# Sampled attention beside a main stream: when keys are turned, when values are gathered, and how the value products stand on TensorE

## The chip, the cores and the metric

The kernel runs on one core of a Trainium2 chip. The metric is device time in microseconds (us) of one execution; below, "before" and "after" are the kernel without and with the change. Engine names in the profile: PE is TensorE (PEld its weight loads), DVE is VectorE, ACT is ScalarE, POOL is GpSimd, SP is SyncE, which here issues most DMAs.

## What is computed

One inference step of a one-layer decoder. A prompt of 2048 new tokens and eight sampled sequences with eight new tokens each go through one input projection, two mixers (FoX attention with forget gates, and an mLSTM with matrix memory), an output projection with layer norm and an MLP with a squared ReLU and a second norm. All data are float32. The part that the change touches is the FoX attention of the sampled tokens over 8192 past tokens per sequence, which lie in pages of 128 tokens, found through a page table:

```python
def _fox_sample(q, k_new, v_new, logf_new, k_past, v_past, logf_past):
    ...
    s_past = jnp.einsum('bqhd,bkhd->bhqk', q, k_past).astype(jnp.float32) * scale
    s_past = s_past + Ln[..., :, None] + R[:, :, None, :]
    s_new = jnp.einsum('bqhd,bkhd->bhqk', q, k_new).astype(jnp.float32) * scale
    ...
    p = jax.nn.softmax(jnp.concatenate([s_past, s_new], axis=-1), axis=-1).astype(v_new.dtype)
    o = jnp.einsum('bhqk,bkhd->bqhd', p[..., :P], v_past) + jnp.einsum('bhqk,bkhd->bqhd', p[..., P:], v_new)
```

Here b is one of 8 sequences, q one of 8 tokens, h one of 8 heads and d one of 64 channels; R is the forget sum from a past token to the end of the past.

## The kernel before, in words

**The main stream.** Four phases follow each other: A (input projection, with the mLSTM beside it), B (prompt attention, `phase_b`), O (output projection, `phase_o`) and C (MLP, `phase_c`). Their large products run in three terms of split numbers through `mm3` (L137 to L140): a high and a low part of each operand, as 128x512 or 128x256 matmuls on the whole 128x128 array.

**The side stream.** The sampled attention is a generator, `sample_attention`, that runs beside phases A, O and C. The main stream calls `tick(us)` after its products with the microseconds that they are thought to take; whenever enough have come together (7.5 us in phase A, 5 us in O and C, never in B), `beside` makes one step of the generator, and the step's instructions on PE, ACT and DVE are put behind the main stream's latest instruction on that engine. A scheduler that works out the order of every engine at build time may still move a step's instructions among the main stream's. On the chip each engine then keeps that order and waits at each instruction for what it needs. POOL and SP are not tied to the main stream: they run ahead until a buffer is not free.

**A step before.** For sequence b, 16 key tiles of 512 tokens are worked through in pairs, each pair in four steps. A step calls `k_step(b, kt, m)` for the current sequence and `pv_step(b - 1, kt + m // 2, m % 2)` for the one before it.

- `k_step` (L1304): a gather from POOL (L1314, an indirect DMA of 512 KB into `kraw`, two buffers), and at once, in the same step, two 128x512 transposes on DVE (L1316) from `kraw` into `kT` (one buffer). The first of four steps also loads the forget sums `Rb` from SP (L1311).
- `qk_step` (L1318), after each fourth step: 16 matmuls of 128x32 weights against 256 columns (L1327); the query tokens of four heads lie in four column quarters of the array, so four matmuls in a row go to four quarters. DVE adds the forget sums and takes the maximum (L1334).
- `softmax` (L1338), after a sequence's last tile: 16 small matmuls (L1345), the maximum, exponentials on ACT, the row sums.
- `weights` (L1381), for each fourth of the tiles: transposes of the weights (L1388) and copies to `PTs` (L1390).
- `pv_step` (L1393): a gather of 512 KB of values into `vt` (L1401, two buffers) and in the same step the four matmuls that use it (L1406), again in four column quarters, all into one accumulator `sO` that is kept for the whole sequence. The last one of a sequence also adds the new tokens' values (L1411) and puts the result out (L1414 to L1423).

So each step has two gathers, and a gather of values may start as soon as PE has used the last value but one. The attention of the last sequence needs one more round of steps without keys.

## Time and profile before

| what | before |
|---|---|
| time, median of 3 runs (lowest to highest) | 3501.9 us (3501.55 to 3503.35) |
| profiled execution: span from first to last instruction | 3492.4 us |
| median of the runs less that span | 9.5 us |
| phase A, from the start | about 1000 us |
| phase B | about 443 us |
| phase O | about 217 us |
| phase C to the end of the sampled attention | about 1300 us |
| the rest of phase C | about 532 us |
| mean granted clock of TensorE | 0.985 |

The profile gives the span of one profiled execution; its time outside the span is not recorded by itself, and the 9.5 us to the median of the runs stand for it. A group row reads: line, engine, operation, out<-in, shape (128*32 means 128 rows and 32 columns of the array), count, busy time and mean ns. A timeline row reads: start and duration in us, engine, line, operation, names, shape, count of equal instructions in a row, and in brackets the engine's idle time before it with what ended it. A float32 matmul of the sampled attention leaves two records, one of the main stream leaves one. A wait row reads: who waited, on which line, for whom, then us in total, number of times and the longest.

### The profile page before, as it was taken

How to read it: one execution, taken by the hardware profiler on the slowest of the kernel's cores; microseconds unless marked ns; L12 is line 12 of the kernel's file. 1: busy time of each engine (PE TensorE's matmuls, PEld its weight loads, DVE VectorE, ACT ScalarE, POOL GpSimd, SP SyncE). 2: the span in 40 equal slices, each digit the busy share in tenths (PEclk: the TensorE clock that was granted, in tenths of full speed). 3: DMA queues.
4: the chain of work that ended last, by engine and by line, in shares of the span. 5: the costliest groups of instructions: out<-in, count | busy, mean ns of one | idle time of the engine just before them, and what ended most of it. 6: DMA issues, size and time to landing. Idle time of an engine off the chain costs nothing.

```text
span 3492.4 us, 59522 instructions
## 1 busy us (share of the span) xinstructions
PE 3354.9 (96%) x22428; PEld 2670.1 (76%) x22428; DVE 2178.9 (62%) x5302; ACT 1366.6 (39%) x2818; POOL 897.4 (26%) x942
## 2 busy tenths in 40 slices
PE   8899899999989999999899999999999999999998
PEld 8898778888866666667567677677677777898887
DVE  6747747657558787655556567666666544654555
ACT  3333323334358888512324243332233333443332
POOL 1013213231322222265332324223324111100000
PEclk9999999999999999999899999999999999999999
DMA  6557777775853232586776767768768555442221
GB/s 198 167 167 223 223 220 237 245 246 174 275 163 86 75 81 57 172 275 215 273 250 197 266 214 262 258 200 271 253 218 296 192 164 176 148 154 73 85 85 64
DMA packets 446040, 663.15 MB, mean 190 GB/s; under 512 B 84604, under 2 KB 333760, under 8 KB 444856
## 3 DMA queue, kind: packets, MB, share of 16 engines
q1 hardware_dynamic: 369064, 380.13, 36.1%
q0 software_dynamic: 74304, 270.57, 22.5%
q10 hardware_dynamic: 2384, 8.65, 0.7%
q8 instruction: 176, 2.88, 0.3%
q14 instruction: 112, 0.92, 0.1%
HBM read 598.01 MB, written 61.22 MB: 189 GB/s over the span
## 4 chain that ended last, share of the span: by engine, by line
PE 69%; DMA 15%; DVE 6%; issue 5%; POOL 3%; ACT 1%; SPq 0%; POOLq 0%; DVEq 0%; ACTq 0%
PE py L138 7%; PE py L140 6%; PE py L139 6%; PE ph L138 6%; PE ph L139 6%; PE ph L140 6%; DMA kraw<-cache_k,idxK 4%; PE po L919 4%; DMA vt<-cache_v,idxV 4%; PE pt L910 4%; PE pm L138 4%; PE pm L139 3%; PE pm L140 3%; PE sO L1406 3%; PE pS L871 2%
## 5 line engine op out<-in xcount | busy, mean ns | idle before, releaser
L1150 DVE TENSOR_TENSOR y<-y,py 128x512 f32<-128x512 f32 (+1 forms) x476 | 319.3, 680 | 251.1 <-PE py L140 246.9
L138 PE MATMUL ph<-x1h,wh 128*128 128x512 f32 (+1 forms) x1280 | 455.5, 356 | 2.4 <-ACT wh L130 2.4
L130 ACT ACTIVATE wh<-wr 128x1024 fp32r<-128x1024 f32 x264 | 273.4, 1057 | 466.0 <-PE py L140 264.0
L139 PE MATMUL ph<-x1l,wh 128*128 128x512 f32 (+1 forms) x1280 | 454.7, 355 | 0.0
L140 PE MATMUL ph<-x1h,wl 128*128 128x512 f32 (+1 forms) x1280 | 453.7, 355 | 0.2 <-DVE wl L133 0.2
L1401 POOL DMA_INDIRECT vt<-cache_v,idxV x256 | 257.9, 1007 | 736.1 <-PE sO L1406 701.2
L1316 DVE STREAM_TRANSPOSE kT<-kraw 128x512 f32<-128x512 f32 x512 | 328.3, 684 | 179.8 <-DMA kraw<-cache_k,idxK 178.4
L138 PE MATMUL py<-wh,hh 128*128 128x512 f32 (+1 forms) x1088 | 431.6, 399 | 1.5 <-DVE y L1148 0.8
L139 PE MATMUL py<-wl,hh 128*128 128x512 f32 (+1 forms) x1088 | 429.6, 395 | 0.7 <-DVE wl L133 0.7
L140 PE MATMUL py<-wh,hl 128*128 128x512 f32 (+1 forms) x1088 | 429.1, 395 | 0.0
L1314 POOL DMA_INDIRECT kraw<-cache_k,idxK x256 | 280.9, 1097 | 571.3 <-DVE kT L1316 439.0
L133 DVE TENSOR_TENSOR wl<-wr,wh 128x1024 fp32r<-128x1024 f32 x264 | 333.2, 1269 | 91.4 <-PE ph L140 25.7
L138 PE MATMUL pm<-whi,xh 128*128 128x256 f32 (+2 forms) x1088 | 320.3, 294 | 7.5 <-DVE st L489 4.8
L139 PE MATMUL pm<-wlo,xh 128*128 128x256 f32 (+2 forms) x1088 | 315.7, 290 | 0.0
L140 PE MATMUL pm<-whi,xl 128*128 128x256 f32 (+2 forms) x1088 | 315.4, 290 | 0.0
L138 PEld LDWEIGHTS ph<-x1h,wh 128*128 128x128 f32 x1280 | 240.9, 188 | 46.5 <-issue 11.1
L140 PEld LDWEIGHTS ph<-x1h,wl 128*128 128x128 f32 x1280 | 240.7, 188 | 42.8 <-issue 11.1
L139 PEld LDWEIGHTS ph<-x1l,wh 128*128 128x128 f32 x1280 | 240.6, 188 | 40.4 <-issue 8.6
L138 PEld LDWEIGHTS py<-wh,hh 128*128 128x128 f32 (+1 forms) x1088 | 201.3, 185 | 62.7 <-issue 18.1
L140 PEld LDWEIGHTS py<-wh,hl 128*128 128x128 f32 (+1 forms) x1088 | 201.3, 185 | 55.5 <-issue 9.9
L139 PEld LDWEIGHTS py<-wl,hh 128*128 128x128 f32 (+1 forms) x1088 | 201.5, 185 | 48.5 <-issue 8.6
L138 PE MATMUL pm<-xh,whi 128*128 128x256 f32 (+1 forms) x768 | 224.7, 293 | 0.8 <-ACT qi L447 0.8
(359 smaller groups left out, 6875.1 us busy)
## 6 DMA issues: line engine op xcount, KB each, us to landing
wr<-w SPq DMA_DIRECT2D x256, 512.0 KB
wra<-w_in SPq DMA_DIRECT2D x112, 512.0 KB
xn<-x_prompt SPq DMA_DIRECT2D x32, 512.0 KB
Rb<-dR SPq DMA_DIRECT2D x128, 128.0 KB
dqk<-th SPq DMA_DIRECT2D x32, 256.0 KB
qk<-dqk SPq DMA_DIRECT2D x16, 512.0 KB
qn<-dq SPq DMA_DIRECT2D x128, 64.0 KB
wr<-w_o SPq DMA_DIRECT2D x16, 512.0 KB
```

Of the source, the lines that this page charges most:

```text
L130: last["ACT"] = A.activation(dst, src, AF.Copy, scale=scale)
L133: r = (eng or V).tensor_tensor(dst, src, hi.bitcast(F32), op=OP.subtract)
L138: T.matmul(ps, wh, xh, start=first, stop=False)
L139: T.matmul(ps, wh, xl, start=False, stop=False)
L140: last["PE"] = T.matmul(ps, wl, xh, start=False, stop=stop)
L910: T.transpose(pt[:, k], sc[i][0][k0 // 4][:, k * 128:(k + 1) * 128], ident)
L919: last["PE"] = T.matmul(po[c:c + 64, q0:], z["vn"][:, k], PT[:, k - k0, q0:], start=(k < 2), stop=(k >= nk - 2), skip_group_check=True)
L1150: V.tensor_tensor(y, y, ps, op=OP.add)
L1314: G.indirect_dma_start(out=kraw, out_offset=None, in_=ck, in_offset=IO(ap=idxK[:, b, kt + k, f:f + 1], axis=0))
L1316: V.transpose(z["kT"][:, k, 2 * f + i].rearrange("p b c -> p (b c)"), kraw[:, i * 512:(i + 1) * 512])
L1401: G.indirect_dma_start(out=vt.rearrange("p f c -> p (f c)"), out_offset=None, in_=cv, in_offset=IO(ap=idxV[:, b, pg * 4 + u, f:f + 1], axi ...
L1406: T.matmul(po[r:r + 32], z["PT"][:, hg, 2 * f + g, pg].rearrange("p h q -> p (h q)"), vt[:, g, hg * 256:(hg + 1) * 256], start=(kt == 0 an ...
```

## The change

The generator's nested loops become a chain of 291 numbered steps, `step(n)`, one for each call by the main stream. In step n:

- the keys that step n - 1 gathered are turned (`k_turn`); every fourth step the score products follow (`qk_step`), and after a sequence's last tile the softmax;
- then the next 512 KB of keys are gathered (`k_gather`, with the load of `Rb` in each fourth step). `kraw` still has two buffers and `kT` one;
- in every second step, the value products of 512 tokens are made (`pv_step`): eight matmuls in place of twice four. The second gathered half comes first (f = 1, then f = 0). `tc.issue_after` puts the first four behind the last score product of the same step, if there is one, and the other four behind the first four;
- right behind them both halves of the next 512 values are gathered (`v_gather`), which the products two steps later use. `vt` still has two buffers. The new tokens' values (`v_new`) are loaded with a sequence's first gather of values instead of in `qk_begin`, and the transposed weights of a fourth of the tiles (`weights`) follow the gather of its first values.

The number of gathers, transposes, matmuls, copies and buffers is the same. `pv_end` is the old end of `pv_step` as a function. Comments and docstrings are gone elsewhere, which moves line numbers and nothing else. The core of the diff:

```diff
-        vn = ps_.tile([8, 512], F32, name="vns", bufs=1)
-        SY.dma_start(vn, O["v_sample"][0, b].rearrange("t h d -> t (h d)"))
...
-    def k_step(b, kt, m):
+    def k_gather(b, j):
         z = state[b]
-        if m == 0:
-            z["kT"] = ps_.tile([128, 2, 4, 16, 32], F32, name="kT", tag="kT", bufs=1)
+        kt, f = j // 2, j % 2
+        z["kraw"] = ps_.tile([128, 1024], F32, name="kraw", tag="kraw", bufs=2)
+        G.indirect_dma_start(out=z["kraw"], out_offset=None, in_=ck, in_offset=IO(ap=idxK[:, b, kt, f:f + 1], axis=0))
+        if j % 4 == 0:
             z["rb"] = ps_.tile([128, 2, 256], F32, name="Rb", bufs=1)
             for hg in range(2):
                 SY.dma_start(z["rb"][:, hg], dap(dR, (b * FH + hg * 4) * PAST + kt * 128, [[2048, 16], [0, 8], [1, 256]]))
-        k, f = divmod(m, 2)
-        kraw = ps_.tile([128, 1024], F32, name="kraw", tag="kraw", bufs=2)
-        G.indirect_dma_start(out=kraw, out_offset=None, in_=ck, in_offset=IO(ap=idxK[:, b, kt + k, f:f + 1], axis=0))
+
+    def k_turn(b, j):
+        z = state[b]
+        if j % 4 == 0:
+            z["kT"] = ps_.tile([128, 2, 4, 16, 32], F32, name="kT", tag="kT", bufs=1)
+        k, f = divmod(j % 4, 2)
         for i in range(2):
-            V.transpose(z["kT"][:, k, 2 * f + i].rearrange("p b c -> p (b c)"), kraw[:, i * 512:(i + 1) * 512])
+            V.transpose(z["kT"][:, k, 2 * f + i].rearrange("p b c -> p (b c)"), z["kraw"][:, i * 512:(i + 1) * 512])
...
-    def pv_step(b, kt, f):
+    def v_gather(b, kt):
         z = state[b]
-        if kt == 0 and f == 0:
+        z["vt"] = []
+        for f in range(2):
+            vt = ps_.tile([128, 2, 512], F32, name="vt", bufs=2)
+            G.indirect_dma_start(out=vt.rearrange("p f c -> p (f c)"), out_offset=None, in_=cv,
+                                 in_offset=IO(ap=idxV[:, b, (kt % 4) * 4 + kt // 4, f:f + 1], axis=0))
+            z["vt"].append(vt)
+
+    def pv_step(b, kt, after):
+        z = state[b]
+        if kt == 0:
             z["po"] = pps.tile([128, 256], F32, name="sO", bufs=1)
         po = z["po"]
-        u, pg = divmod(kt, 4)
-        vt = ps_.tile([128, 2, 512], F32, name="vt", bufs=2)
-        G.indirect_dma_start(out=vt.rearrange("p f c -> p (f c)"), out_offset=None, in_=cv,
-                             in_offset=IO(ap=idxV[:, b, pg * 4 + u, f:f + 1], axis=0))
-        for g in range(2):
-            for hg in range(2):
-                r = (g * 2 + hg) * 32
-                T.matmul(po[r:r + 32], z["PT"][:, hg, 2 * f + g, pg].rearrange("p h q -> p (h q)"),
-                         vt[:, g, hg * 256:(hg + 1) * 256], start=(kt == 0 and f == 0),
-                         stop=(g == 1 and kt == 15 and f == 1), skip_group_check=True)
+        pg = kt % 4
+        for n, f in enumerate((1, 0)):
+            with ExitStack() as es:
+                if after is not None:
+                    es.enter_context(tc.issue_after(after.ins))
+                for g in range(2):
+                    for hg in range(2):
+                        r = (g * 2 + hg) * 32
+                        after_ = T.matmul(po[r:r + 32], z["PT"][:, hg, 2 * f + g, pg].rearrange("p h q -> p (h q)"),
+                                          z["vt"][f][:, g, hg * 256:(hg + 1) * 256], start=(kt == 0 and n == 0),
+                                          stop=(g == 1 and kt == 15 and n == 1), skip_group_check=True)
+            after = after_
+        if kt == 15:
+            pv_end(b, po)
...
-    yield 1
-    for b in range(9):
-        if b < 8:
-            qk_begin(b)
-        for kt in range(0, 16, 2):
-            if b > 0 and kt % 4 == 0:
-                weights(b - 1, kt // 4)
-            for m in range(4):
-                yield 1
-                if b < 8:
-                    k_step(b, kt, m)
-                if b > 0:
-                    pv_step(b - 1, kt + m // 2, m % 2)
-            if b < 8:
-                qk_step(b, kt)
+    def step(n):
+        after = None
+        b, j = divmod(n, 32)
+        kb, kj = divmod(n - 1, 32)
+        vb, vj = divmod(n - 36, 32)
+        if 0 <= kb < 8:
+            k_turn(kb, kj)
+            if j % 4 == 0:
+                after = qk_step(kb, kj // 4 * 2)
+                if j == 0:
+                    softmax(kb)
         if b < 8:
-            softmax(b)
+            if j == 0:
+                qk_begin(b)
+            k_gather(b, j)
+        if n % 2 == 0:
+            if 0 <= vb < 8:
+                pv_step(vb, vj // 2, after)
+            wb, wj = divmod(n - 34, 32)
+            if 0 <= wb < 8:
+                v_gather(wb, wj // 2)
+                if wj == 0:
+                    v_new(wb)
+                if wj % 8 == 0:
+                    weights(wb, wj // 8)
+
+    for n in range(36 + 8 * 32 - 1):
+        yield 1
+        step(n)
```

More of the change, by code (lines that the diff above doesn't have):

```diff
@@ L1326, in qk_step @@
                     hd = (hg * 4 + h4) * 2 + db
[L1327 to L1328 removed]
+                    r = T.matmul(pq[h4 * 32:h4 * 32 + 32, hg], z["qb"][:, hd], kv[:, :, hd],
+                                 start=(db == 0), stop=(db == 1), skip_group_check=True)
         if kt % 4 == 0:
```

40 lines of the change are left out of this document (21 added, 19 removed).

## The prediction

> **What bounds the kernel now.** I read the profile's page first, then busy time by stage, then what was waited for, and last TensorE's timeline around single instructions.
>
> ```profile
> span 3492.4 us, 59522 instructions
> PE 3354.9 (96%) x22428; PEld 2670.1 (76%) x22428; DVE 2178.9 (62%) x5302; ACT 1366.6 (39%) x2818; POOL 897.4 (26%) x942
> ```
>
> PE is busy for 96% of the span; no other engine passes 62%. The table by stage gives PE first, then weight loads, DVE, ACT, POOL, the granted clock and the share of the DMA engines:
>
> ```profile
> 0.00:1000.00 1000.00, 924.82 (x7716) 847.12 (x7717) 627.81 (x1752) 333.00 (x722) 241.74 (x260) 0.98 0.70 214
> 1000.00:1443.00 443.00, 436.00 (x3012) 302.44 (x3010) 345.83 (x1374) 366.92 (x1025) 115.08 (x192) 0.99 0.30 80
> 1443.00:1660.00 217.00, 209.96 (x1198) 154.20 (x1202) 120.54 (x261) 50.68 (x72) 127.25 (x100) 0.97 0.79 259
> 1660.00:2960.00 1300.00, 1269.10 (x7558) 916.12 (x7547) 789.50 (x1499) 422.55 (x687) 391.51 (x377) 0.99 0.70 233
> 2960.00:3492.40 532.40, 515.02 (x2956) 450.19 (x2954) 295.19 (x418) 193.41 (x314) 21.84 (x15) 0.99 0.33 102
> ```
>
> The rows are phases A, B, O, C while the sampled attention runs, and C after it. The attention's steps stand in rows one, three and four; in all three PE is busy for 92 to 98% at nearly full clock. So a step is worth what it takes from PE's own time. Who waits in it:
>
> ```profile
> POOL vt L1401 <- PE sO L1406: 701.2, 158, 53.7
> POOL kraw L1314 <- DVE kT L1316: 439.0, 147, 15.2
> DVE kT L1316 <- DMA kraw<-cache_k,idxK: 178.4, 75, 8.2
> PEld sO L1406 <- DMA vt<-cache_v,idxV: 41.0, 36, 5.6
> PE sO L1406 <- DMA vt<-cache_v,idxV: 25.6, 24, 5.2
> PE sQ L1327 <- DVE kT L1316: 6.0, 5, 3.6
> ```
>
> POOL's 701 and 439 us and DVE's 178 us are idle time of engines with room. What reaches PE is 25.6 us (41.0 on the weight loads) for values, and 6.0 us for turned keys. Those waits are small; the larger cost is hidden in PE's busy time, and only the timeline shows it.
>
> **What a switch of tile shape costs.** The score and value products use 32 columns of the array (128*32): four of them, on four column quarters, run side by side. I call four such matmuls a group; each matmul has two records, so a group is x8.
>
> ```profile
> 1936.35 0.39 PE L138 MATMUL ph<-x1h,wh 128*128 128x512 f32 x1
> 1936.58 0.39 PE L139 MATMUL ph<-x1l,wh 128*128 128x512 f32 x1
> 1936.90 0.64 PE L1406 MATMUL sO<-vt,PTs 128*32 128x256 f32 x8
> 1937.47 0.50 PE L140 MATMUL ph<-x1h,wl 128*128 128x512 f32 x1
> 1937.80 0.40 PE L138 MATMUL ph<-x1h,wh 128*128 128x512 f32 x1
> ```
>
> A main matmul follows the last after 0.23 us (1936.35 to 1936.58). From 1936.58 to 1937.80 are 1.22 us, with two main matmuls in it: the lone group cost 1.22 - 0.45 = 0.77. The group starts 0.32 after the matmul before it, and the first full one behind it takes 0.33 instead of 0.23.
>
> ```profile
> 2060.08 0.39 PE L139 MATMUL ph<-x1l,wh 128*128 128x512 f32 x1
> 2060.40 1.93 PE L1327 MATMUL sQ<-kT,qb 128*32 128x256 f32 x32
> ...
> 2062.60 0.40 PE L139 MATMUL py<-wl,hh 128*128 128x512 f32 x1
> ```
>
> Sixteen score products in a row are four groups: 2.52 - 0.45 = 2.07. So a further group in the same stretch costs (2.07 - 0.77) / 3 = 0.43, and a stretch costs 0.77 - 0.43 = 0.34 for being entered and left.
>
> ```profile
> 1944.96 0.39 PE L139 MATMUL ph<-x1l,wh 128*128 128x512 f32 x1
> 1945.28 0.40 PE L1327 MATMUL sQ<-kT,qb 128*32 128x256 f32 x1
> ...
> 1948.38 0.39 PE L138 MATMUL ph<-x1h,wh 128*128 128x512 f32 x1
> ```
>
> This stretch holds sixteen score and eight value products, mixed by the scheduler: 3.42 - 0.45 = 2.97; the two prices give 0.34 + 6 x 0.43 = 2.92. They hold for mixtures of both kinds. A part of a group costs as much as a whole one, as a single matmul (x2) shows with 1.20 - 0.45 = 0.75:
>
> ```profile
> 2100.99 0.39 PE L140 MATMUL py<-wh,hl 128*128 128x512 f32 x1
> 2101.30 0.62 PE L1406 MATMUL sO<-vt,PTs 128*32 128x256 f32 x2
> ...
> 2102.19 0.39 PE L139 MATMUL py<-wl,hh 128*128 128x512 f32 x1
> ```
>
> **The change, part by part.** *Value products chained.* I counted in the order in which the two built programs put PE's instructions; PE keeps it. Before, the 2064 wide matmuls of this kind lie in 299 stretches (with the narrow ones of the softmax); 155 of them are one value group alone, 37 a single value matmul. After, there are 179: 72 are a chain of eight value products, 34 are sixteen score products with the chain behind them. That is 120 stretches fewer: 120 x 0.34 = 40.8 us. Groups that were torn apart are whole again: counted as column quarters allow, 588 groups become 533, and 55 x 0.43 = 23.7 us. The number of matmuls is the same, so these 64.5 us are pure savings of PE. Nothing hid them: PE's next full matmul stands behind every stretch.
>
> *Prompt attention.* It contains no step of the sampled attention, but the scheduler orders it anew: its 64-column products (L919) lie in 115 stretches where there were 132.
>
> ```profile
> 1304.29 0.27 PE L910 MATMUL pt<-ident,S 128*128 128x128 f32 x1
> 1304.49 1.08 PE L919 MATMUL po<-PT,vn 128*64 128x256 f32 x8
> 1305.51 0.44 PE L910 MATMUL pt<-ident,S 128*128 128x128 f32 x2
> ```
>
> One transpose and four products take 1.22; a transpose alone takes about 0.11 (0.44 for two with its end), two rounds of products 2 x 0.43, so a stretch costs some 0.25: 17 x 0.25 = 4 us gained, an estimate between 0 and 17 x 0.34 = 6.
>
> *Values gathered in pairs, two steps ahead.* Buffers and gathers are as many as before; what changes is how long a gather has before PE needs it. Before, a gather is issued when the last group but one has read its buffer. By the built order and the prices above, phases O and C leave a median of 9.1 us from there to the use (a tenth below 7.6, five of 208 below 3). After, both gathers wait for the whole chain of eight, and the next chain stands a median of 10.2 us behind its end (a tenth below 9.0; two of 104 below 2, one of them at none). So there is 1 us more. But the second gather, which the chain uses first, goes out 1.25 us after the first:
>
> ```profile
> 2232.22 0.94 POOL L1314 DMA_INDIRECT kraw<-cache_k,idxK  x1 [3.05 <-DVE kT L1316]
> 2233.47 0.94 POOL L1314 DMA_INDIRECT kraw<-cache_k,idxK  x1 [0.30 <-DVE kT L1316]
> 2237.74 1.31 DVE L1316 STREAM_TRANSPOSE kT<-kraw 128x512 f32<-128x512 f32 x2 [0.56 <-DMA kraw<-cache_k,idxK]
> 2239.81 1.30 DVE L1316 STREAM_TRANSPOSE kT<-kraw 128x512 f32<-128x512 f32 x2 [0.77 <-DMA kraw<-cache_k,idxK]
> ```
>
> Here two gathers of the same size landed 5.5 and 6.3 us after their issue, each with a reader waiting. At the other end, a second gather was waited for much longer:
>
> ```profile
> 2160.00 0.94 POOL L1401 DMA_INDIRECT vt<-cache_v,idxV  x1 [0.30 <-issue]
> 2169.47 0.64 PE L1406 MATMUL sO<-vt,PTs 128*32 128x256 f32 x8 [1.15 <-DMA vt<-cache_v,idxV]
> ```
>
> 9.5 us. POOL starts a gather 0.30 us after what frees it (the rows with 0.30). After a chain's end, 0.30 + 1.25 + 6.3 = 7.9 us is well below the 10.2 us that there are; with 9.5 it is 11.05, and PE waits 0.85. Chains are half as many as groups were, and each that waits does so for longer. The two short ones would cost about 8 and 6 us (7.9 less what they have), where before the five below 3 cost about 3 each. I set the change of this term at 0. It can't gain more than the 41.0 us that there are; with every second gather at 9.5 us it would lose 104 x 0.85 + 14 - 33 = 69 (33 is the middle of the two rows above, 25.6 and 41.0).
>
> [...]
>
> *Keys turned a step behind their gather.* DVE's 178 us of waiting should mostly go, with POOL's 439. PE sees 6.0 us of it; behind a transpose that waits stand evictions on DVE, but PE's waits for those stand below the last of the rows shown. I take 0, between 0 and +6 gained. *New values loaded later*: eight small transfers on SP, 0. *v waits behind q*: the chain behind sixteen score products waits with PE's main stream behind it; that is the gather's term.
>
> **Sum.** 3492.4 - 40.8 - 23.7 - 4 = 3423.9 us of span. The median of the runs, 3501.9, is 9.5 above the profiled span; so 3433.
>
> **Rivals.** (1) *The waits for values go altogether*, as gathers have 1 us more: 33 less, 3400. For: the medians. Against: the row with 9.5 us. [...] (2) *Waits grow*: second gathers are often near 9.5 us, not 6.3; half of the loss worked out above, +35: 3468. For: POOL puts a key gather ahead of the two, three in one queue. (3) *PE is no longer the bound*: the main stream, 4% denser, waits for weights. Half of the 68.5 us is lost: 3467. Against: in the fourth row DMA has 0.70, DVE 0.61 (789.5 / 1300). (4) *Slower*: the second gather is late in every chain. A mean wait w adds 104 w + 14 - 33; it eats the 68.5 us at w = 0.84, a mean latency of 10.2 + 0.84 - 1.55 = 9.5 us. At 10 us, w = 1.35 and the time is 3433 + 121 = 3554. Only the longest of the rows quoted reaches that point. (5) *Chains are not formed*: excluded by the built order, up to the few that are torn (seven single value matmuls are left).
>
> **Chances.** Forecast 0.62 (3418 to 3448), (1) 0.14, (2) 0.12, (3) 0.06, (4) 0.05 and 0.01 for the rest. The range takes in (1) to (3): 3395 to 3475. About 0.2%, 7 us, is what a measurement of this kernel can tell from no change; slower by more 0.05, within it 0.04, faster 0.91.
>
> **What will show it.** Right: in the profile after, value products as x16 behind one entry of 0.32 us; the busy time of sO and sQ together down by some 40 to 65 us; PE's waits for values still 20 to 45 us, in fewer and longer pieces; DVE's wait for key gathers far below 178 us. The stage from phase O to the end of the sampled attention, 1517 us before, shortens by about 50. Wrong: waits of PE for values above 100 us; or stretches as chained as I say but the main stream's matmuls further apart than 0.23.

## The result, and the profile after

The changed kernel took 3524.3 us, the median of four runs (3519.6 to 3528.7); the kernel before took 3502.6 beside it. The ratio is 1.0071, 95% interval 1.0049 to 1.0092: slower by some 25 us (21.6 between these two medians), where 3433 was forecast and 3475 was the upper end. The profiled run is the slowest of the four, 3528.7 us. Its page begins with the span and the busy times:

```profile
span 3527.0 us, 59546 instructions
PE 3320.9 (94%) x22428; PEld 2700.9 (77%) x22428; DVE 2182.2 (62%) x5302; ACT 1369.4 (39%) x2818; POOL 891.7 (25%) x942
```

PE is busy for 34.0 us less than before (3354.9), and yet the span is 34.6 us longer: PE's idle time, span less busy, went from 137.5 to 206.1 us. But in every later run with a recorded span the time is only 1.7 us above the span, so most of the 9.5 us between span and median before was no time outside the span: the profiled execution of the kernel before was some 8 us faster than its other runs, and that of the changed kernel is its slowest. About 13 of the 34.6 us come from this; the forecast of 3433 is not touched by it, as it is the median less 68.5. By stage (the same columns as before; the rows are phase A, phase O up to the MLP's first product, and C from there to the end of the sampled attention):

```profile
0.00:1017.00 1017.00, 927.88 (x7711) 862.05 (x7712) 626.67 (x1754) 334.16 (x726) 242.88 (x258) 0.96 0.69 210
...
1460.00:1718.00 258.00, 228.77 (x1388) 170.80 (x1386) 146.17 (x312) 60.97 (x88) 150.09 (x117) 0.94 0.80 268
1718.00:3005.00 1287.00, 1232.93 (x7454) 926.00 (x7456) 777.87 (x1464) 424.40 (x682) 363.90 (x360) 0.99 0.69 228
```

These rows have other bounds than those ahead of the prediction. With the same bounds in both traces (the first product of the next phase), phase A went from 1003.8 to 1016.7 us, phase O from 258.2 to 258.8, C to the end of the sampled attention from 1257 to 1287, and the rest from 533 to 521. Phase O to the end of the sampled attention (rows two and three) takes 1545 us. Before, the same stretch, from its first product to the last value product, took this:

```profile
1443.60:2958.90 1515.30, 1477.96 (x8744) 1069.61 (x8744) 908.88 (x1758) 472.62 (x757) 518.28 (x475) 0.99 0.71 237
```

So it grew by 30 us, though PE is busy for 16 us less in it. It also holds 98 of PE's instructions more, 83 of them of the main stream, which stood behind it before; from phase O to the end of the kernel the changed one is 19 us longer, and 16 us ahead of phase O. The view of the waits shows what grew most:

```profile
DVE kT L1320 <- DMA kraw<-cache_k,idxK: 202.7, 86, 6.9
PE sO L1427 <- DMA vt<-cache_v,idxV: 52.6, 22, 8.8
PE px L262 <- DMA xn<-x_prompt: 15.4, 5, 5.0
PE sQ L1331 <- DVE kT L1320: 9.6, 8, 3.6
```

PE's wait for values has doubled, 25.6 to 52.6 us, in fewer and longer pieces. The products themselves did what was forecast. A chain of eight value products alone, then one behind sixteen score products:

```profile
2414.73 0.39 PE L139 MATMUL py<-wl,hh 128*128 128x512 f32 x1
2415.05 1.07 PE L1427 MATMUL sO<-vt,PTs 128*32 128x256 f32 x16
...
2416.39 0.40 PE L138 MATMUL py<-wh,hh 128*128 128x512 f32 x1
...
2430.31 0.39 PE L138 MATMUL ph<-x1h,wh 128*128 128x512 f32 x1
2430.63 1.93 PE L1331 MATMUL sQ<-kT,qb 128*32 128x256 f32 x32
2432.38 1.05 PE L1427 MATMUL sO<-vt,PTs 128*32 128x256 f32 x16
...
2433.70 0.40 PE L139 MATMUL py<-wl,hh 128*128 128x512 f32 x1
```

1.66 - 0.45 = 1.21 and 3.39 - 0.45 = 2.94, where the two prices give 1.20 and 2.92.

**Where a long wait comes from.** GpSimd's instructions beside a chain of eight whose last product ended at 2444.21 (2443.14 + 1.07), and the next chain:

```profile
2443.14 1.07 PE L1427 MATMUL sO<-vt,PTs 128*32 128x256 f32 x16
2445.43 0.95 POOL L1307 DMA_INDIRECT kraw<-cache_k,idxK  x1 [7.42 <-DVE kT L1320]
2446.69 0.95 POOL L1307 DMA_INDIRECT kraw<-cache_k,idxK  x1 [0.32 <-DVE kT L1320]
2447.95 1.00 POOL L1408 DMA_INDIRECT vt<-cache_v,idxV  x1 [0.30 <-issue]
2449.26 1.43 POOL L1408 DMA_INDIRECT vt<-cache_v,idxV  x1 [0.30 <-issue]
2458.99 1.94 PE L1427 MATMUL sO<-vt,PTs 128*32 128x256 f32 x16 [3.80 <-DMA vt<-cache_v,idxV]
```

Both value buffers were free at 2444.21. But GpSimd stood at a key gather that waited 7.42 us for VectorE's transposes; the value gathers behind it left 3.7 and 5.1 us after the chain's end, and TensorE waited 3.80 us. Chain by chain in the trace, 30.0 of the 52.6 us were waited by 14 chains of this kind: GpSimd was held at one or two key gathers by VectorE's transposes, and the second value gather left 2.4 to 6.3 us after the chain's end, where it leaves 1.1 us after it if nothing holds it. The two short chains of the prediction waited 17.1 us, six others 5.6.

**What a pause brings besides.** The clock (the number ahead of the DMA share) in TensorE's longest pause, a wait of 8.83 us for values, and behind it:

```profile
1696.50:1705.30 8.80, 0.01 (x3) 0.02 (x3) 7.49 (x10) 6.48 (x8) 4.86 (x4) 0.74 0.89 298
1705.30:1718.00 12.70, 6.62 (x36) 4.58 (x36) 3.89 (x5) 3.06 (x5) 2.21 (x2) 0.50 0.87 314
1718.00:1725.00 7.00, 6.67 (x16) 4.98 (x17) 1.29 (x2) 0.77 (x2) 0.00 (x0) 0.53 0.64 219
```

For 19 us after the pause the products run at half clock. So I count a third thing beside price and idle time: the **lost clock**, half of the time at granted clock 0.5 that lies outside TensorE's pauses of over 0.3 us, added up from the trace's record of the clock (4 to 6 us of each figure lie behind TensorE's last product and cost nothing). This gives an account that holds for all of the kernel's variants below: busy time less the price of the built stretches and groups (0.34 and 0.43 each, unrounded 0.337 and 0.433) less the lost clock is 2948 to 2962 us in each of the seventeen profiles.

| kernel | ratio to before (95%) | price | span | PE busy | PE idle | lost clock | PE waits for values |
|---|---|---|---|---|---|---|---|
| before | 1 | 355 | 3492.4 | 3354.9 | 137.5 | 46 | 25.6, 24 times |
| changed | 1.0071 (1.0049 to 1.0092) | 291 | 3527.0 | 3320.9 | 206.1 | 73 | 52.6, 22 |
| e1 keys in their step | 1.0077 (1.0056 to 1.0098) | 330 | 3510.1 | 3334.4 | 175.7 | 56 | 60.0, 30 |
| e2 values as before | 1.0027 (1.0016 to 1.0037) | 361 | 3496.2 | 3355.1 | 141.1 | 44 | 26.5, 20 |
| e3 not chained | 1.0121 (1.0104 to 1.0138) | 323 | 3526.7 | 3338.9 | 187.8 | 66 | 51.4, 27 |
| e4 values first in the queue | 1.0358 (1.0338 to 1.0379) | 282 | 3626.9 | 3330.7 | 296.2 | 88 | 105.6, 37 |
| e5 third buffer | 0.9910 (0.9885 to 0.9935) | 289 | 3444.8 | 3297.5 | 147.3 | 47 | 19.5, 15 |
| e6 its memory, two buffers | 1.0132 (1.0109 to 1.0154) | 296 | 3519.3 | 3318.5 | 200.8 | 66 | 68.3, 26 |
| e7 changed, no value wait | 0.9855 (0.9833 to 0.9876) | 281 | 3430.2 | 3286.5 | 143.7 | 51 | 0 |
| e8 before, no value wait | 1.0025 (1.0011 to 1.0039) | 335 | 3479.3 | 3332.5 | 146.8 | 45 | 0 |
| e9 before, third buffer | 1.0016 (1.0003 to 1.0029) | 356 | 3484.8 | 3356.4 | 128.4 | 47 | 17.2, 18 |
| e10 third, keys in their step | 0.9944 (0.9925 to 0.9963) | 332 | 3460.6 | 3322.3 | 138.3 | 42 | 8.4, 10 |
| e11 third, not chained | 0.9919 (0.9899 to 0.9939) | 320 | 3450.2 | 3316.8 | 133.4 | 46 | 7.5, 4 |
| e14 third, gathers alternate | 1.0009 (0.9993 to 1.0025) | 288 | 3497.4 | 3310.2 | 187.2 | 63 | 25.8, 13 |
| e15 before, other order | 1.0041 (1.0024 to 1.0059) | 356 | 3507.0 | 3351.7 | 155.3 | 43 | 24.0, 22 |
| e16 changed, other order | 1.0046 (1.0029 to 1.0063) | 292 | 3508.5 | 3315.4 | 193.1 | 62 | 54.2, 24 |
| e17 third, other order | 0.9912 (0.9894 to 0.9930) | 286 | 3473.1 | 3306.9 | 166.2 | 60 | 16.3, 11 |

Ratios are to runs of the kernel before on the same chip, where it took 3490, 3481, 3484, 3486 and 3494 us in the later sets; spans of different rows may come from different chips, and each is one execution, up to 12 us away from its kernel's median (e17). From before to changed the account reads: price -64, idle +68.6, lost clock +27, the rest +3: together the 34.6 us of the span.

### The profile page after: what moved, and what is told of

It reads as the page before. It is cut to its first block, busy times and chain, and to the rows that moved or that the text cites. A ratio compares the mean times of both kernels' runs of the same rounds, so it can differ in the third digit from the quotient of the medians.

```text
span 3527.0 us, 59546 instructions
## 1 busy us (share of the span) xinstructions
PE 3320.9 (94%) x22428; PEld 2700.9 (77%) x22428; DVE 2182.2 (62%) x5302; ACT 1369.4 (39%) x2818; POOL 891.7 (25%) x942
## 4 chain that ended last, share of the span: by engine, by line
PE 43%; DMA 16%; issue 9%; DVE 5%; POOL 2%; ACT 2%; SPq 0%; another core or an unknown queue 0%; POOLq 0%; ACTq 0%; DVEq 0%
DMA vt<-cache_v,idxV 6%; DMA kraw<-cache_k,idxK 5%; PE py L138 4%; PE py L140 4%; PE py L139 4%; PE ph L139 4%; PE ph L140 4%; PE ph L138 4%; PE po L919 4%; PE pt L910 3%; PE pS L871 2%; PE sO L1427 2%; PE pS L872 2%; DMA wr<-w 1%; POOL vt L1408 1%
## 5 line engine op out<-in xcount | busy, mean ns | idle before, releaser
L1320 DVE STREAM_TRANSPOSE kT<-kraw 128x512 f32<-128x512 f32 x512 | 328.0, 685 | 203.2 <-DMA kraw<-cache_k,idxK 202.7
L1307 POOL DMA_INDIRECT kraw<-cache_k,idxK x256 | 273.1, 1067 | 574.8 <-DVE kT L1320 408.2
L1122 ACT ACTIVATE hq<-ph 128x512 f32<-128x512 f32 (+1 forms) x160 | 82.8, 518 | 387.8 <-PE ph L140 339.0
```

What stands on the lines that cost most here:

```text
L1122: A.activation(hq, ps, AF.Relu)
L1307: G.indirect_dma_start(out=z["kraw"], out_offset=None, in_=ck, in_offset=IO(ap=idxK[:, b, kt, f:f + 1], axis=0))
L1320: V.transpose(z["kT"][:, k, 2 * f + i].rearrange("p b c -> p (b c)"), z["kraw"][:, i * 512:(i + 1) * 512])
```

## The experiments

**Theory 1**: the values are late. Two buffers and a chain that reads both mean that no gather leaves before the chain's end; then it may stand behind a key gather in GpSimd's queue; what TensorE waits, it pays again in lost clock. **Theory 2**: the step by which keys are turned later is what costs. **Theory 3**: the order that came out at building, of the main stream too, was unlucky.

**The parts one by one, with two buffers.** e1 takes the keys' part back:

```diff
-        if 0 <= kb < 8:
-            k_turn(kb, kj)
-            if j % 4 == 0:
-                after = qk_step(kb, kj // 4 * 2)
...
             k_gather(b, j)
+            k_turn(b, j)
+            if j % 4 == 3:
+                after = qk_step(b, j // 4 * 2)
+                if j == 31:
+                    softmax(b)
```

> The changed kernel with its keys turned and scored in the step of their gather, as before the change; the values stay gathered in pairs and chained. By the built order and the prices of the prediction (0.34 us a stretch, 0.43 a group) the sampled products cost 330 us here, against 355 before and 291 after the change. Theory 1 (the waits come from the values: both gathers of a pair leave only when the whole chain is done, and then stand in GpSimd's queue behind a key gather, and every long wait is followed by a stretch at half clock): the waits stay as in the changed kernel, so the time is its 3524 plus 39, some 3560. Theory 2 (what costs is that the keys are turned a step behind): the waits go back to those of before, so the time is 3503 less 25, some 3478. Theory 3 (the built order of the main stream happened to come out worse, in the input projection above all): anything within 15 us of 3500.

e2 takes the values' part back (gather and four products in one step, no chain) and keeps the keys':

```diff
-        if n % 2 == 0:
-            if 0 <= vb < 8:
-                pv_step(vb, vj // 2, after)
...
-                v_gather(wb, wj // 2)
+        if 0 <= vb < 8:
...
+            pv_step(vb, vj // 2, vj % 2)
```

> The keys as changed (turned a step behind their gather), the values as before: each gather and its four products in one step, no chain. The built order has 306 stretches and 597 groups, 361 us by the prices of the prediction against 355 before. Theory 1 (late values in pairs): the waits are those of before, so 3503 plus 6, some 3509. Theory 2 (keys a step behind): the waits of the changed kernel come with the keys, some 100 us of them with the lost clock, so 3600 or close to it. Theory 3 (luck of the built order): 3503 plus 6, give or take 15.

e3 only drops the orders that hold the chain together:

```diff
-                if after is not None:
-                    es.enter_context(tc.issue_after(after.ins))
```

> The changed kernel without the two orders that chain the products: the pairs of gathers stay. 213 stretches and 582 groups, 323 us by the prices of the prediction, 33 more than the changed kernel. Theory 1: the gathers leave as late as in the changed kernel, the waits stay, and the time is 3524 plus 33, some 3557. If the chain itself makes the waits, as its eight products come up at once and release both buffers late, the waits fall by half and the time is some 3510.

Measured: e1 1.0077, e2 1.0027, e3 1.0121. e2 is as theory 1 had it (its 6 us more of price are most of its 9 us) and rules out that the keys alone cost 100 us. e1 keeps all of the value waits (60.0 us) without the keys' step, so they come with the pairs. But e1 was to be 39 us slower than the changed kernel and is level with it: turning keys a step behind saves 39 us of price there, and gives as much back. e3 is slower than the changed kernel by 0.5%, 18 us, where the price is 33 more; if the luck of the built order (below) is left aside, chaining gives back about half. Theory 1 is right on the values and leaves something out.

**GpSimd's order.** e4 queues each even step's key gather behind the two value gathers (`last` is the second of them):

```diff
-            k_gather(b, j)
...
+                if b < 8:
+                    with tc.issue_after(last.ins):
+                        k_gather(b, j)
```

> The changed kernel with GpSimd's order fixed: in each even step the key gather is queued behind the two value gathers, so that these leave as soon as the chain is done, and the key gather 2.5 us later than it did. 154 stretches and 532 groups, 282 us by the prices of the prediction, 9 less than the changed kernel. Theory 1: the product waits for values fall from 53 us to 15 or less, the half-clock stretches from 190 us to some 110, and the time is 3524 less 9, 38 and 35, some 3440. Theory 2: the keys are later still, VectorE's waits for them (203 us) and TensorE's for turned keys grow, and the time is 3524 or more.

Measured: 1.0358, the worst of all. Most of it is one stretch near the end of the sampled attention, here by stage over 120 us:

```profile
2985.00:3105.00 120.00, 37.32 (x278) 14.20 (x278) 3.78 (x13) 3.60 (x14) 28.08 (x30) 0.53 0.40 131
```

and two chains of it in TensorE's timeline:

```profile
3063.52 1.94 PE L1428 MATMUL sO<-vt,PTs 128*32 128x256 f32 x16 [6.12 <-DMA vt<-cache_v,idxV]
3071.57 1.93 PE L1428 MATMUL sO<-vt,PTs 128*32 128x256 f32 x16 [6.11 <-DMA vt<-cache_v,idxV]
```

In the fixed order the steps ran behind the main stream, and the last 16 chains stand in PE's order where the main stream waits for the sampled tokens: one chain per 8.05 us, of which 6.1 are the wait for its own gathers, at half clock. VectorE's waits for key gathers went to 379 us. So my expectation failed, and the run can't tell what the order does while there is main work: the 75 chains before that waited 20.5 us against 34.6 in the changed kernel (8.8 of these in one of its two short chains), but stood 16.6 us apart instead of 15.0.

**A third value buffer.** e5 has three value buffers. The 4 KB come from small tiles: the constant triangle, the q rows of the beginning, the new values and the scaled output share one buffer, the q and mask tiles of a sequence and some of the softmax have one instead of two, and the row selectors are stored without half of their zeros. e6 has the same tiles and two value buffers:

```diff
-            vt = ps_.tile([128, 2, 512], F32, name="vt", bufs=2)
+            vt = ps_.tile([128, 2, 512], F32, name="vt", bufs=3)
...
-        qt = ps_.tile([128, 2, 16, 8], F32, name="qt", bufs=2)
+        qt = ps_.tile([128, 2, 16, 8], F32, name="qt", bufs=1)
...
-        os_ = ps_.tile([128, 256], F32, name="os", bufs=1)
+        os_ = ps_.tile([128, 256], F32, name="os", tag="vns", bufs=1)
```

> The changed kernel with a third value buffer, so that the first gather of a pair needn't wait for the chain before it; the 4 KB come from sharing and halving small tiles of the sampled attention. 165 stretches and 539 groups, 289 us by the prices of the prediction, 2 less than the changed kernel. Theory 1 (late values, then half clock): the product waits for values fall from 53 us to some 15 and the half-clock stretches from 190 us to some 120, so the time is 3524 less 2, 38 and 35, some 3450. Rival (the second gather of the pair, which still leaves after the chain, is the one that lands last): half of that, some 3490. Theory 2 (keys a step late): no better than 3515.

> The control of the third buffer: the same sharing of small tiles, but two value buffers as in the changed kernel. 184 stretches and 540 groups, 295 us by the prices of the prediction, 5 more than the changed kernel. Theories 1 and 2: the changed kernel's time and 5, some 3529. Theory 3 (luck of the built order): up to 15 away from that either way.

Measured: e5 0.9910, e6 1.0132; e5 is faster than both kernels. e6 is 0.6%, 21 us, slower than the changed kernel, where the price is 5 more: that is beyond the 15 us that I had allowed for the order's luck. Against the changed kernel itself e5 gains 1.6%. e5 and e6 differ in the third buffer (and in what order the building made of it), by 2.2%. e5's page, and its and e6's row of the value waits:

```profile
span 3444.8 us, 59513 instructions
PE 3297.5 (96%) x22428; PEld 2683.0 (78%) x22428; DVE 2175.8 (63%) x5301; ACT 1367.5 (40%) x2818; POOL 892.3 (26%) x942
```

```profile
PE sO L1427 <- DMA vt<-cache_v,idxV: 19.5, 15, 4.9
```

```profile
PE sO L1427 <- DMA vt<-cache_v,idxV: 68.3, 26, 8.5
```

Of the 74.5 us between the spans, 48.8 are value waits (all of the idle time that goes is 53.5), 18.3 lost clock and 6.9 price, together 4 more than the spans differ by. This is theory 1 with both its halves: with each microsecond of value wait went 0.4 us of clock. What the buffer changes stands in GpSimd's rows of e5:

```profile
1643.58 0.96 POOL L1408 DMA_INDIRECT vt<-cache_v,idxV  x1 [0.59 <-PE sO L1427]
1648.76 0.94 POOL L1307 DMA_INDIRECT kraw<-cache_k,idxK  x1 [4.22 <-DVE kT L1320]
1650.01 0.95 POOL L1408 DMA_INDIRECT vt<-cache_v,idxV  x1 [0.30 <-issue]
```

A chain's end frees one gather that goes at once, and the other of the pair, which has a buffer already, may stand behind the key gather. The gather that the next chain needs last is issued up to 0.13 us before or after the chain's end in three chains of four in e5; in the changed kernel the median is 1.26 us behind, and a quarter of the chains have 4.17 or more.

**No product waits for values.** e7 is the changed kernel, e8 the one before, with the value products on a constant tile (so the sampled outputs leave the values out, and all gathers still run):

```diff
-                                          z["vt"][f][:, g, hg * 256:(hg + 1) * 256], start=(kt == 0 and n == 0),
+                                          sel.rearrange("p a b c -> p (a b c)"), start=(kt == 0 and n == 0),
```

> The changed kernel with its value products reading a constant tile in place of the gathered values; the gathers still run, but no product waits for them, so the sampled tokens' outputs leave the values out. 145 stretches and 537 groups, 281 us by the prices of the prediction, 10 less than the changed kernel. Theory 1: the waits of 53 us and the half clock behind them go, so 3524 less 10, 53 and about 40, some 3420. Theory 2 (keys a step late): the waits move to the keys and the time stays above 3480.

> The kernel before, with the same cut: its value products read a constant tile, the gathers run on, and the sampled outputs leave the values out. 245 stretches and 584 groups, 335 us by the prices of the prediction, 20 less than before. Theory 1: 3503 less 20, 26 of waits and some 10 of lost clock, some 3447; the changed kernel without value waits is then 30 to 54 us faster than this one. If the prices of a stretch and a group were too high, the two would be alike.

Measured: 0.9855 and 1.0025. e7 is as expected within 0.9% (3452 for 3420, on a scale where before takes 3503). For e8 I had 3447 and it came to 3511, even above the kernel before. By stage, ahead of phase O and from it to the end, e7 first:

```profile
0.00:1467.90 1467.90, 1359.60 (x10710) 1161.39 (x10710) 981.02 (x3126) 702.75 (x1748) 577.04 (x660) 0.96 0.76 244
1467.90:3430.20 1962.30, 1926.88 (x11718) 1528.55 (x11718) 1201.28 (x2177) 664.06 (x1071) 323.96 (x282) 0.99 0.48 155
```

and e8:

```profile
0.00:1478.20 1478.20, 1368.38 (x10727) 1161.20 (x10727) 979.80 (x3126) 702.47 (x1748) 573.17 (x660) 0.97 0.75 243
1478.20:3479.30 2001.10, 1964.07 (x11702) 1526.25 (x11702) 1196.20 (x2177) 664.71 (x1071) 330.97 (x282) 0.99 0.47 152
```

Ahead of phase O both lose 24 to 35 us against the 1443.6 of before: no product holds the value gathers back, so all 256 are issued there (48 in the kernel before), and the two kernels are no clean subtraction. From phase O on, e8 takes 2001.1 us and e7 1962.3; 38.8 us, and the built stretches and groups of that part cost 38.3 us less by the prices. Where no value is waited for, the change is worth what the prices say; this part of both kernels has no value gathers beside it either.

**The parts again, with three buffers.** e9 is the kernel before, e10 is e1, e11 is e3, each with the third buffer as in e5 (e9 also loads a sequence's new values at its first value step).

> The kernel before with a third value buffer (and the new values loaded at a sequence's first value step, without which the shared tiles don't fit). 295 stretches and 594 groups, 356 us by the prices of the prediction against 355 before. All times here on a scale on which the kernel before takes 3503. Theory 1 (late values): most of the 26 us of value waits go and 10 us of lost clock with them, some 3475 to 3485. Rival (the third buffer is all that made the changed kernel with three buffers fast, 0.991 of before; steps and chain bring nothing): 3471 or less.

> Third value buffer, values in chained pairs, keys turned and scored in the step of their gather. 224 stretches and 592 groups, 332 us by the prices of the prediction, 43 more than the changed kernel with three buffers (0.991 of before, 3471 on a scale where before takes 3503). Theory 1: 3471 plus 43, some 3514. Theory 2 (keys a step behind cost some 40 us of waits, as they seemed to with two buffers: the changed kernel has 39 us less of product time than the one with keys in their step and is no faster): some 3475.

> Third value buffer and the changed kernel's steps, but without the orders that chain the products. 198 stretches and 586 groups, 320 us by the prices of the prediction, 31 more than the changed kernel with three buffers (0.991 of before, 3471 on a scale where before takes 3503). By those prices some 3502. If the chain gives back what it saves (its eight products wait for the later of two gathers), some 3475.

Measured: 1.0016, 0.9944, 0.9919. The kernel before gains nothing from the buffer, so the rival that it alone makes e5 fast falls, and so does my 20 us for e9: its value waits went from 25.6 to 17.2 us only. The pairs bring 0.7% (e9 to e10), all three parts 1.1% (to e5). But each part gives less than its price: e10 to e5 is 43 us of price and 0.34%, 12 us; e11 to e5 is 31 us and no difference that the intervals allow to tell (0.9919 and 0.9910). In e11 TensorE waits 7.5 us for values, in e5 19.5, and its idle time is 14 us less: chained, eight products wait for the later of two gathers. Some 11 us more of e5's busy time the prices don't cover.

**The prices by themselves.** e12 and e13 are kernels of their own; `main(n)` is n products of 128x512, `side(n)` n column-tiled value products. e12:

```diff
+    for n in SIDES:
+        for _ in range(12):
+            main(24)
+            side(n)
```

and e13, where every block of products reads what VectorE copied, and the first copy reads what the last product wrote:

```diff
+            V.tensor_copy(ev[:, 0:128], pm[(199 if first else 239) % 3][:, 0:128])
+            n = int(us * 960)
+            while n > 0:
+                V.tensor_copy(ev[:, 0:min(n, 7680)], ev[:, 0:min(n, 7680)])
+                n -= 7680
+            x = p.tile([128, 512], F32R, name="x2", bufs=2)
+            V.tensor_copy(x, ev[:, 0:512])
+            main(240, x)
```

> A kernel of its own that computes none of the outputs: products of 128x512 in a row, first with 0, 4, 8, 16 and 24 column-tiled value products after every 24 of them (12 times each), then with pauses in which TensorE waits for VectorE, from some 1 us to some 17 us, each after 150 products and three times. By the prices of the prediction a repetition with n value products takes 0.34 plus 0.43 for each 4 more than one without: 0.77, 1.20, 2.07 and 2.93 us. Theory 1's second half: every pause over some 2.5 us is followed by 3 to 24 us at half clock, none under 2 us is, and the products in that stretch take twice their time. If half clock came of something else, the pauses would leave the clock at 1.

> A kernel of its own that computes none of the outputs: 240 products of 128x512 in a row, then a pause in which TensorE waits for copies of VectorE, 39 times, with pauses from some 1 us to some 14 us in 13 steps of three each. Each block's products read what the copies wrote, so that they can't begin before. Theory 1's second half: every pause over some 2.5 us is followed by 3 to 24 us at half clock, which cost half their length; none under 2 us is. If half clock came of something else (the transfers, other engines), the clock stays at 1.

Measured in e12, the starts of the first two stretches with 4 value products and of the first two with 16:

```profile
128.33 0.42 PE L83 MATMUL sO<-vt,PT 128*32 128x256 f32 x4
134.57 0.42 PE L83 MATMUL sO<-vt,PT 128*32 128x256 f32 x4
...
291.22 0.42 PE L83 MATMUL sO<-vt,PT 128*32 128x256 f32 x4
298.74 0.42 PE L83 MATMUL sO<-vt,PT 128*32 128x256 f32 x4
```

A repetition takes 6.24 and 7.52 us; less 24 main products at 0.227 (5.45 us), a stretch costs 0.79 and 2.07 us, for 0.77 and 2.07 expected. With 8 and 24 products it is 1.25 and 2.99 (6.70 and 8.44 us a repetition), for 1.20 and 2.93. The prices are right. e12's pauses never came, as VectorE's copies ran ahead (TensorE's only wait for VectorE is 10.6 us before the first products), so it says nothing on the clock. In e13 they came, 180.1 us of waits for VectorE in all. The first products after five of the pauses, each with its wait in brackets:

```profile
394.23 2.11 PE L78 MATMUL py<-x,wh 128*128 128x512 f32 x8 [1.54 <-DVE x L91]
563.43 1.59 PE L78 MATMUL py<-x,wh 128*128 128x512 f32 x4 [2.04 <-DVE x L91]
1330.02 1.22 PE L78 MATMUL py<-x,wh 128*128 128x512 f32 x2 [4.04 <-DVE x L91]
1831.13 1.22 PE L78 MATMUL py<-x,wh 128*128 128x512 f32 x2 [7.23 <-DVE x L91]
2229.79 1.65 PE L78 MATMUL py<-x,wh 128*128 128x512 f32 x3 [13.43 <-DVE x L91]
```

and ten microseconds behind each of these five, with PE's busy time, the clock, and the share and GB/s of the DMA engines:

```profile
394.30:404.30 10.00, 10.00 (x44) 1.00 0.00 0
563.50:573.50 10.00, 10.00 (x37) 0.83 0.01 2
1330.10:1340.10 10.00, 10.00 (x33) 0.73 0.00 0
1831.20:1841.20 10.00, 10.00 (x32) 0.70 0.00 0
2229.90:2239.90 10.00, 10.00 (x38) 0.84 0.00 0
```

In ten microseconds TensorE starts 44 products after a pause of 1.54 us and 32 after one of 7.23. Hardly a transfer runs there (0.00 or 0.01 of the DMA engines' time, up to 2 GB/s), and in the two of these stretches where all engines were read, behind 1.54 and 4.04 us, VectorE and GpSimd are busy for 0.00 us: what differs ahead of the five is the length of the wait for VectorE's copies. So in e13 the half clock came with the pause and not with transfers or other engines' work.

**Alternate gathers.** e14 has e5's buffers, and GpSimd's order fixed to one value gather, one key gather; keys are gathered two in each odd step, behind the latest value gather (`lastv`):

```diff
-            k_gather(b, j)
+        for g in (n, n + 1) if n % 2 else ():
+            if g < 256:
+                with ExitStack() as es:
+                    if lastv:
+                        es.enter_context(tc.issue_after(lastv[-1].ins))
+                    k_gather(*divmod(g, 32))
```

> The changed kernel with three value buffers, and GpSimd's order fixed to one value gather, one key gather, alternately (two key gathers are issued in each odd step, behind the value gathers). 163 stretches and 540 groups, 288 us by the prices of the prediction, as with three buffers before (0.991 of the kernel before). If a key gather that stands ahead of a value gather in GpSimd's queue is what makes it late, nearly every second value gather is late now: the value waits rise from 20 us to 40 or more and the time to 1.00 of before. If what counts is that the second gather leaves only after the chain, the time stays at 0.991.

Measured: 1.0009, so it loses all that e5 has, as the theory of the key gather in front had it; but not for its reason, as the value waits are 25.8 us and not 40. The idle time is 40 us above e5's, spread over many rows, and VectorE waits 317 us for key gathers instead of 207. In its trace only 7 of 105 second gathers left more than 2 us after a chain's end (43 of 105 in the changed kernel, 4 in e5), so with three buffers a key gather in front rarely holds them; what costs the 1% instead was not settled.

**Another built order.** The same three kernels with one constant changed, which shifts where the steps fall:

```diff
-PACE_A = 7.5
+PACE_A = 7.4
```

> A control: the kernel before, with a step of the sampled attention for every 7.4 us of the main stream's products in the first phases in place of 7.5; nothing else is changed, but the built order comes out otherwise (303 stretches and 586 groups, 356 us by the prices of the prediction, 1 more than before). If the built order's luck is worth up to 15 us (theory 3), the ratio may be anywhere from 0.996 to 1.004; if not, it is 1.000.

> The same control for the changed kernel: 180 stretches and 536 groups, 292 us by the prices of the prediction, 2 more than the changed kernel. Theory 1 (late values through two buffers): 1.007 of before as the changed kernel, with some 50 us of value waits. Theory 3 (luck of the built order makes the changed kernel slow): it may as well come out under 1.000.

> The same control for the changed kernel with a third value buffer: 162 stretches and 535 groups, 286 us by the prices of the prediction, 3 less than it had. Theory 1: 0.990 of before, with some 20 us of value waits. Theory 3: anywhere up to 1.000.

Measured: 1.0041, 1.0046, 0.9912. The order is worth 0.4%, 14 us, to the kernel before, and -0.25% to the changed one: in this order the two take the same time. So theory 3 is right in its size, and no difference of less than some 15 us above is put down to a step. What holds in both orders is that 64 us of price bring nothing with two buffers (value waits 52.6 and 54.2 us) and 0.9% (against before in its own order, 1.3%) with three (19.5 and 16.3).

## Why the prediction was wrong

Forecast were 3423.9 us of span, and it was 3527.0, 103 us more (91 between the 3433 and the median of the runs). The account splits these into 68.6 of idle time (forecast: none), 27 of lost clock (not in the sum at all), and 7 of busy time (forecast -68.5, measured -34.0 with the 27 us of lost clock in it, so -61).

- **Value products chained, prompt attention: right.** The prices hold for a chain (1.21), a chain behind scores (2.94), by themselves (e12), and in a stage without value waits (38.8 us for 38.3). Busy time of sO and sQ fell from 343.3 (192.5 + 150.8) to 277.1 us, by 66, just over the 40 to 65 forecast; that of the prompt attention's products (L919) fell from 153.0 to 149.3, by the 4 us of the sum, though the phase as a whole got no shorter (442.9 us for 439.8):

```profile
L1427 PE MATMUL sO<-vt,PTs 128*32 128x256 f32 x2048 | 147.7, 394 | 52.7 <-DMA vt<-cache_v,idxV 52.6
L1331 PE MATMUL sQ<-kT,qb 128*32 128x256 f32 x2048 | 129.4, 386 | 11.2 <-DVE kT L1320 9.6 <-ACT PTs L1395 1.6
```

- **The step that failed: "After a chain's end, 0.30 + 1.25 + 6.3 = 7.9 us is well below the 10.2 us that there are", and so "I set the change of this term at 0".** The room was there (a median of 10.4 us from a chain's end to where the next one stands, 11.3 with the waits) and the latency nearly (6.6 us for the last gather, a tenth over 8.1). The issue was not: the sum has GpSimd free when the chain ends. In a quarter of the chains the second gather left 4.17 us or more behind it, and of the 52.6 us that were waited, 30.0 stand behind key gathers that waited for VectorE. I had the rival for it ("POOL puts a key gather ahead of the two, three in one queue"), gave it 0.12, and priced only latency. The two short chains came as foreseen (waits of 8.8 and 8.2 us for "about 8 and 6"). The 0.30 us were misread: in the rows they are GpSimd's idle time between two gathers. A gather that nothing holds starts as the chain ends, and the second 1.1 us later, for 1.55 in the sum; this error was to the safe side.
- **The price of a wait.** A wait was counted as its own length. It took lost clock with it, 0.4 us for each microsecond between e6 and e5 (18.3 for 48.8); so by an estimate with this ratio the 27 us of value waits are some 37 of the 103.
- **Keys a step behind: wrong in what it does, nearly right in what it costs alone.** VectorE's wait for key gathers did not go; it is 202.7 us for 178.4 (154.2 in e2, where only the keys moved). Alone it costs 0.27% (e2), within the luck of the order. Beside pairs it gives back most of the price that it saves (39 us between e1 and the changed kernel, 43 between e10 and e5). Why was not shown; a key gather can only leave when the buffer is turned, and that comes a step later too.
- **What the list of signs missed.** It named "waits of PE for values above 100 us" as what would prove it wrong; 52.6 were enough. The sum also took all other idle time as unchanged, without a reason. It grew by some 40 us: 12.6 in phase A, 3.4 in B, 6.5 behind the sampled attention, the rest in O and C. It is spread over many of PE's waits, of which only that for x_prompt grew by as much as 10 us (5.4 to 15.4), in phase A; a share of it is the order's luck, as e6, with the same steps, has phase A end at 997.6 us and not at 1016.7.
- **Rivals.** (2) had the mechanism and 3468; (4) decided at a mean wait of 0.84 us a chain, and the 106 chains from phase O on had 0.50, the two short ones included (52.7 us): TensorE lost there less than the chain saves, and the clock and the spread waits did the rest. The first built order had its part too: in the second, the changed kernel is as fast as the one before, still without the gain.

## What to carry to other kernels

Before work is gathered in larger pieces, count from when each buffer is free, not from when the data are needed: the changed kernel loses 0.7% with two buffers (nothing in the second built order, against the kernel before in its own) and wins 0.9% with a third (1.3%), which the kernel before had no use for. Look also at what stands ahead in the queue that issues the transfer, since a wait there delays all behind it (7.42 us at a key gather put two value gathers 3.7 and 5.1 us behind the chain's end). Where TensorE sets the time, a pause can cost more than its length (in e13 the ten microseconds behind 2.04 us ran at a clock of 0.83, behind 1.54 us at 1.00), and a gain or loss of under half a per cent should be tried in a second built order before it is believed.

## What the runs showed of the hardware

- The clock after a pause, in e13 as its rows above have it: in the ten microseconds behind a pause of 1.54 us it was 1.00, behind 2.04 us 0.83, behind 4.04, 7.23 and 13.43 us 0.73, 0.70 and 0.84. Half clock followed all three pauses of 2.04 us there, but one of three of 2.54 us and one of three of 3.04.
- In the two kernels' own traces 27 of the changed kernel's 28 pauses of 2.5 us or more were followed by half clock within 2 us, for 3.4 to 23.9 us; behind the other one, a wait of 2.99 us for values that ended at 1527.90, the clock was 1.00 for 9.4 us. In the kernel before it was 8 of 11; behind the other three, of 2.80, 3.63 and 3.60 us (ended at 162.3, 302.6 and 742.8), the clock of the next ten microseconds was 1.00. So the expectation, half clock after every pause over some 2.5 us and none under 2, held only in part.
- A part of the half clock fell into the pause itself, where no product runs: the 8.8 us of the changed kernel's longest pause have a clock of 0.74. Behind that pause of 8.83 us half clock lasted 19 us (0.50 and 0.53 in the rows), with further waits in it (TensorE is busy for 6.62 of 12.70 us).
- A switch between full-array and column-tiled products cost 0.34 us a stretch in the kernel and 0.36 in e12 (0.79 less 0.43), and the rows show no wait in it: it shows only as a later start (0.32 us, for 0.23 between full products) and one longer product (0.50 us for 0.39).
